# Layer a's last four attention pairs: three couples of contraction tiles in seven products, and a softmax without the row's own gate sum

## The chip, the cores and the metric

The kernel runs on one core of one Trainium2 chip. The metric is the device time of one launch in microseconds (us); three runs of the kernel before gave 2052.01, 2052.78 and 2052.95 us.

## The reference, cut to what matters

Two transformer layers over 256 rows of 2048 numbers, all in float32. Layer a projects to queries, keys, values and a forget gate, attends causally with a bias that is the difference of two running sums of log gates, projects back, and runs a squared-ReLU MLP. Layer b does the same with chunked attention and a learned relative bias. The change is in layer a's projection and attention:

```python
u = rms_norm(h, a_norm_g[l])
proj = u @ a_w_in[l]                      # 256 x 2048 times 2048 x (3*2048 + 16)
q, k, v, fz = jnp.split(proj, [D, 2 * D, 3 * D], axis=-1)
...
logf = jax.nn.log_sigmoid(fz + a_b_f[l])
c = jnp.transpose(jnp.cumsum(logf, axis=1), (0, 2, 1))
...
s = jnp.einsum('bqhd,bkhd->bhqk', qb, kb).astype(jnp.float32) * scale
s = s + c[:, :, q0:q1, None] - c[:, :, None, :q1]
s = jnp.where(causal[None, None], s, -jnp.inf)
p = jax.nn.softmax(s, axis=-1).astype(vb.dtype)
```

The term `c[:, :, q0:q1, None]` is one number per query row; a softmax over the row gives the same result without it.

## The kernel before, in words

**Precision.** Every large product is made three times: each float32 operand is split into a part `hi` that TensorE multiplies in its float32r format and a rest `lo`, and hi·hi, hi·lo and lo·hi are summed. For the weights the split is made on the chip: ScalarE copies a loaded weight tile into `hi` (L323), VectorE subtracts to get `lo` (L324). A weight tile is 128 partitions by 1024: two contraction tiles of 128 by 512 output columns.

**Units.** The program is a long list of units that TensorE works off in written order. A *plain unit* is one weight tile: 2 contraction tiles, 2 halves of the 256 rows, 3 passes, so 12 matmuls of 128x128x512 (L592, L594, L596: the first two passes use `hi`, the third uses `lo`). Panels of 512 output columns are taken in pairs, and a pair needs 16 contraction tiles for each of its two panels.

**Seven products.** In a pair, part of the contraction is done by the seven-product scheme for 2x2 block matrices instead of eight block products. The four blocks are called 11, 12, 21 and 22; sums of blocks T1 to T4 are needed, and a *form* is one of the seven products, in the order 11, T3, T2, T1, 21, T4, 22. T3 = 22 + 12 and T2 = T3 + 11 are made by VectorE (`make`, L970); T1 = 12 + 11 and T4 = T2 + 21 are made by a DMA that adds from HBM into the tile (`put`, L980, on GpSimd's queue). The matching sums of activations lie in tiles `S` (L395 to L405). A *couple* is one contraction tile of the blocks 1x with one of 2x. Attention pairs do two couples in seven products: a form is 6 matmuls, the seven are 42 in place of 48, and the other 12 contraction tiles take 6 plain units for each panel. Pairs of the MLP do four couples, each form in two parts.

**Order.** `Pair.plan` writes the units of a pair in a row, with plain units between forms by the strings of the table ORD ("a3" is plain unit 3 of the first panel, "b4" unit 4 of the second, "F" the next form). `run` follows the list. Ahead of the products of a unit, `top_up` splits the weights of the next ones: at most three `hi`/`lo` pairs exist (pool `wsp`, 3 buffers), and raw weight tiles are loaded about three ahead on the queue of SyncE. After each unit `run` calls `run_fill` as many times as the table HM says; each call issues one slot of other work: head norms, transposes, softmaxes, value products. Tables such as HS say how many plain units ahead of a pair's first form its blocks are loaded and its sums made, in the order 12, 22, 21, 11, T3, T1. A written order is kept on VectorE, ScalarE, TensorE and SyncE, and for GpSimd's arithmetic.

**Layer a's attention.** Twelve panels (four groups of query, key, value) in six pairs: the first pair is plain units only, five follow with two couples each (order "qkv"), then two pairs of the output projection ("out0", "out1"), then the MLP. From the MLP on every fifth weight tile that is loaded, counted from the program's start, goes into a tile of pool tag `z`, which the hidden activations' transposes also use. The softmax of one head (four to a group) works on two halves, 128x128 and 128x256. For each half VectorE adds the scores, the row's own gate sum `cq` and the bias tile (`scalar_tensor_tensor`, L738) and then takes the row maximum (`tensor_reduce`, L740); ScalarE takes the exponential (L746), and VectorE scales by the reciprocal (L749, L751) and transposes (L440). Layer b has no `cq`: there one `tensor_tensor_reduce` for each half (L742) adds, negates and takes the minimum at once. `cq` is made once by two TensorE transposes (L902) and a copy.

## Time and profile before

| what | value |
|---|---|
| median of three runs | 2052.78 us (2052.01 to 2052.95) |
| the profiled execution, its own time | 2049.66 us |
| its span from first to last instruction | 2047.9 us |
| granted TensorE clock, mean | 0.999 |
| attention of layer a in the trace, with the output projection | up to about 425 us |

The page gives for each engine the time in which it was busy; matmuls are pipelined, so that a reported 390 ns of one matmul overlaps the next. The spacing of starts is read from the chain of work that ended last and from the timeline. Idle time of an engine counts only where TensorE, which works nearly all the time, waits for it.

### The profile page before, as it was taken

Reading aid. Unit: us, or ns where it says so; the run is one execution under the profiler, and the core shown is the slowest. Engines: PE = TensorE matmul, PEld = TensorE weight load, DVE = VectorE, ACT = ScalarE, POOL = GpSimd, SP = SyncE. Lnnn points to the kernel's source line nnn. Section 1 sums busy time; section 2 is a strip of 40 time slices with the busy share of each in tenths; the row PEclk is TensorE's granted clock in tenths of the full one; section 3 lists DMA queues with packets and bytes.
Section 4 is the critical chain, followed back from the end, with each engine's and each line's share of the span. In section 5 each row is a group of like instructions: output and inputs, shape, how many; then the busy total and the mean of one; then the engine's idle time right before and its main releaser. Section 6 shows DMA issues by size and latency. Waiting matters only on the chain.

```text
span 2047.9 us, 27097 instructions
## 1 busy us (share of the span) xinstructions
PE 2041.1 (100%) x9062; PEld 1688.5 (82%) x9062; DVE 1783.5 (87%) x2065; ACT 1403.7 (69%) x1805; POOL 245.0 (12%) x351
## 2 busy tenths in 40 slices
PE   9999999999999999999999999999999999999999
PEld 7888888888888888888888888888888888888887
DVE  7788888998898899899988778888988998988996
ACT  7766666677677677677778666667766676776764
POOL 1111110011111102101012111001101111111020
PEclk9999999999999999999999999999999999999999
DMA  8898888998888898898879888888988888888984
GB/s 322 265 298 272 266 280 243 309 278 272 282 262 281 272 293 272 247 292 273 260 242 311 275 254 287 255 264 284 291 291 265 266 270 284 266 284 261 299 259 147
DMA packets 175309, 557.78 MB, mean 272 GB/s; under 512 B 40624, under 2 KB 69184, under 8 KB 152640
## 3 DMA queue, kind: packets, MB, share of 16 engines
q1 hardware_dynamic: 154112, 464.99, 63.9%
q0 software_dynamic: 20768, 90.75, 22.5%
q8 instruction: 71, 1.16, 0.2%
q14 instruction: 70, 0.57, 0.1%
q10 hardware_dynamic: 288, 0.30, 0.1%
HBM read 516.07 MB, written 27.29 MB: 265 GB/s over the span
## 4 chain that ended last, share of the span: by engine, by line
PE 98%; DVE 1%; ACT 1%; issue 0%; DMA 0%; DVEq 0%; ACTq 0%
PE acc L596 23%; PE acc L592 23%; PE acc L594 23%; PE s L592 9%; PE s L594 9%; PE s L596 9%; PE po L729 1%; PE po L766 1%; DVE lo L324 0%; PE po L767 0%; PE po L728 0%; ACT hi L323 0%; DMA gsb<-in_gs 0%; PE pg L868 0%; DVE s L995 0%
## 5 line engine op out<-in xcount | busy, mean ns | idle before, releaser
L324 DVE TENSOR_TENSOR lo<-raw,hi 128x1024 fp32r<-128x1024 f32 (+1 forms) x409 | 493.5, 1211 | 81.5 <-ACT hi L323 77.1
L323 ACT ACTIVATE hi<-raw 128x1024 fp32r<-128x1024 f32 (+1 forms) x409 | 429.5, 1054 | 194.0 <-PE acc L594 123.4
L592 PE MATMUL acc<-hi,act 128*128 128x512 f32 x1774 | 496.3, 393 | 0.7 <-ACT hi L323 0.7
L596 PE MATMUL acc<-lo,act 128*128 128x512 f32 x1774 | 491.1, 390 | 0.7 <-DVE lo L324 0.6
L594 PE MATMUL acc<-hi,act 128*128 128x512 f32 x1774 | 490.7, 389 | 0.0
L596 PEld LDWEIGHTS acc<-lo,act 128*128 128x128 f32 x1774 | 332.5, 188 | 72.1 <-DVE lo L324 3.1
L594 PEld LDWEIGHTS acc<-hi,act 128*128 128x128 f32 x1774 | 333.0, 188 | 70.1 <-DVE act L383 0.5
L592 PEld LDWEIGHTS acc<-hi,act 128*128 128x128 f32 x1774 | 331.2, 188 | 69.6 <-ACT hi L323 2.1
L323 ACT ACTIVATE hi<-w 128x1024 fp32r<-128x1024 f32 x254 | 267.0, 1058 | 124.0 <-PE acc L594 82.7
L324 DVE TENSOR_TENSOR lo<-wT,hi 128x1024 fp32r<-128x1024 f32 x220 | 267.2, 1221 | 66.1 <-ACT hi L323 62.2
L324 DVE TENSOR_TENSOR lo<-w,hi 128x1024 fp32r<-128x1024 f32 x254 | 305.3, 1217 | 14.0 <-ACT hi L323 12.3
L323 ACT ACTIVATE hi<-wT 128x1024 fp32r<-128x1024 f32 x220 | 232.1, 1059 | 102.1 <-PE acc L594 48.5
L592 PE MATMUL s<-hi,act 128*128 128x512 f32 x530 | 146.3, 391 | 0.0
L596 PE MATMUL s<-lo,act 128*128 128x512 f32 x530 | 145.0, 389 | 0.0
L594 PE MATMUL s<-hi,act 128*128 128x512 f32 x530 | 144.8, 388 | 0.0
L466 POOL DMA_DIRECT2D q<-z x192 | 95.7, 510 | 255.1 <-DVE z L440 211.0
L596 PEld LDWEIGHTS s<-lo,act 128*128 128x128 f32 x530 | 99.2, 188 | 20.8 <-DVE lo L324 0.5
L594 PEld LDWEIGHTS s<-hi,act 128*128 128x128 f32 x530 | 99.4, 188 | 20.6
L592 PEld LDWEIGHTS s<-hi,act 128*128 128x128 f32 x530 | 99.1, 188 | 20.2
L592 PE MATMUL s<-hi,S 128*128 128x512 f32 x288 | 89.6, 392 | 0.0
L596 PE MATMUL s<-lo,S 128*128 128x512 f32 x288 | 88.8, 390 | 0.0
L594 PE MATMUL s<-hi,S 128*128 128x512 f32 x288 | 88.7, 389 | 0.0
(217 smaller groups left out, 2284.4 us busy)
## 6 DMA issues: line engine op xcount, KB each, us to landing
raw<-in_w_in SPq DMA_DIRECT2D x75, 512.0 KB, 5.9
w<-in_w2fa SPq DMA_DIRECT2D x32, 1024.0 KB, 6.5
w<-in_w2fb SPq DMA_DIRECT2D x32, 1024.0 KB, 6.2
w<-in_w1fa SPq DMA_DIRECT2D x27, 1024.0 KB, 7.0
w<-in_w1fb SPq DMA_DIRECT2D x27, 1024.0 KB, 7.3
raw<-in_w2sa SPq DMA_DIRECT2D x52, 512.0 KB, 7.0
raw<-in_w2sb SPq DMA_DIRECT2D x50, 512.0 KB, 7.3
raw<-in_w_kv SPq DMA_DIRECT2D x48, 512.0 KB, 5.1
```

The costliest lines, as they stand in the source:

```text
L323: S.activation(hi[:, c], raw[:, c], AF.Copy)
L324: V.tensor_tensor(lo[:, c], raw[:, c], hi[:, c].bitcast(F32), op=ALU.subtract)
L466: (G if i % 2 else SY).dma_start(dst[32 * j : 32 * j + 32, i * n : (i + 1) * n], z[32 * i : 32 * i + 32, j * n : (j + 1) * n])
L592: TE.matmul(ps[:, cols], xh, cut(hi, j), start=first, stop=False, **kw)
L594: TE.matmul(ps[:, cols], xl, cut(hi, j), start=False, stop=False, **kw)
L596: TE.matmul(ps[:, cols], xh, cut(lo, j), start=False, stop=last, **kw)
L729: TE.matmul(s[:, P : 3 * P], q[:, a, P:T], k[:, a], start=True, stop=True)
L766: TE.matmul(po[:, :T], v[:, 0, a * P : (a + 1) * P], pT[:, :2], start=True, stop=False)
```

## The change

1. The last four attention pairs (order "three") do three couples, six contraction tiles, in seven products. Their blocks are 128x1536 (`WIDE`). Each form has a first part of 1024 columns (6 matmuls) and a second, a *half form*, of 512 (3 matmuls); 5 plain units for each panel are left instead of 6. The columns 1024 to 1536 of the four blocks lie beside the others in two tiles of their own (`beside`: a tile `aside` of pool tag "s", and the first half of `h[0]`, which held x and is loaded again from HBM when "out0" opens). T3 and T2 become two VectorE additions each, T1 and T4 two DMAs each.
2. A half form's `hi` and `lo` come from the same three full-size buffers and count as split ahead like any other. Before, halves of this size would have had a buffer of their own; no pair had any.
3. One further sum of activations (`sum_third`) for the third couple, once, early.
4. The softmax of layer a takes layer b's form, one `tensor_tensor_reduce` per half; `cq` and its two transposes are gone.
5. Tables: HM has 153 numbers in place of 133 with the same sum, 113; the pairs "three" get the row "a3 a4 F a5 F a6 b3 a7 F b4" and the times HT, "out0" gets (9, 8, 1, 6, 6, 5).

```diff
-    "HM": (1, 2, 1, 0, 0, 1, 1, 1, 0, 1, 1, 2, 1, 1, 0, 1, 1, 1, 1, 1, 2, 0, 1, 1, 1, 1, 1, 0, 1, 0, 0, 1, 1, 1, 0, 0, 1, 1, 1, 1, 0, 1, 1, 1, 1, 1,
+    "HM": (1, 2, 1, 0, 0, 1, 1, 1, 0, 1, 1, 2, 1, 1, 0, 1, 1, 1, 1, 0, 1, 2, 0, 1, 1, 0, 1, 1, 0, 1, 0, 1, 0, 0, 1, 0, 1, 1, 0, 0, 0, 1, 1, 0, 1, 1,
...
+    "HT": (7, 8, 1, 5, 4, 3),
...
-    "OFH": (11, 10, 2, 7, 7, 6),
+    "OFH": (9, 8, 1, 6, 6, 5),
...
-        "deep0": "a4 F F F b4 a5 a6 a7"},
+        "deep0": "a4 F F F b4 a5 a6 a7", "three": "a3 a4 F a5 F a6 b3 a7 F b4"},
...
+        if three is not None:
+            f, s = three
+            for i in range(f.shape[0] // 4):
+                src = [[None] * 3 + [s[5 * (2 * i + q) + u] for u in range(5)] for q in range(2)]
+                big = {k: f[4 * i + m] for m, k in enumerate(("11", "12", "21", "22"))}
+                j = len(pairs) + 1
+                pairs.append(Pair(big, src, "three", j % 2 == 1, TABLES["HT" if i else "HS"], WIDE))
...
-        hi = wsp.tile([P, n], F32R, name="hi" if n == UN else "hih", bufs=3 if n == UN else 1)
-        lo = wsp.tile([P, n], F32R, name="lo" if n == UN else "loh", bufs=3 if n == UN else 1)
+        hi = wsp.tile([P, UN], F32R, name="hi", bufs=3)[:, :n]
+        lo = wsp.tile([P, UN], F32R, name="lo", bufs=3)[:, :n]
...
-        ready.append((hi, lo, n < UN))
+        ready.append((hi, lo, False))
...
-        tag = "qs"[g // 2]
+        tag = "qs"[g // 2 if layer else 0]
...
-            if cq is not None:
-                V.scalar_tensor_tensor(t[:, c], s[:, c], cq[:, b, g * GH + a : g * GH + a + 1], bias[:, a, c],
-                                       op0=ALU.add, op1=ALU.add)
-                V.tensor_reduce(nm[:, b : b + 1], t[:, c], axis=AX.X, op=ALU.max, negate=True)
-            else:
-                V.tensor_tensor_reduce(out=t[:, c], in0=s[:, c], in1=bias[:, a, c], scale=-1.0, scalar=-3.0 * NEG,
-                                       op0=ALU.add, op1=ALU.min, accum_out=nm[:, b : b + 1])
+            V.tensor_tensor_reduce(out=t[:, c], in0=s[:, c], in1=bias[:, a, c], scale=-1.0, scalar=-3.0 * NEG,
+                                   op0=ALU.add, op1=ALU.min, accum_out=nm[:, b : b + 1])
...
+            if p.wide:
+                p.e[name] = beside(p.rooms[name])
+                SY.dma_start(p.e[name], p.big[name][:, UN:])
...
         V.tensor_tensor(d, a, b, op=ALU.add)
+        if e:
+            V.tensor_tensor(*e, op=ALU.add)
...
         G.dma_start(p.t[name][:, cols], p.big[other][:, cols], accum_op=ALU.add)
+        if p.e:
+            G.dma_start(p.e[name], p.big[other][:, UN:], accum_op=ALU.add)
...
+    def sum_third(x, fs):
+        y = wk.tile([P, 512], F32, name="y3", tag="wk").rearrange("p (a t) -> p a t", a=2)
+        for j in range(2):
+            V.tensor_tensor(y[:, j], x[2 * UA + j][:, 0].bitcast(F32), x[2 * UA + j][:, 1].bitcast(F32), op=ALU.add)
+        yield
+        s = qkv.tile([P, UN], F32R, name="S", tag="s", bufs=2)
+        fs.extend(s[:, i * 512 : i * 512 + 512] for i in range(2))
+        yield from sums([[y[:, j : j + 1, b * P : (b + 1) * P] for j in range(2)] for b in range(NB)], fs[2:], 1)
...
+            if p.order == "out0" and three:
+                SY.dma_start(h[0][:, :UN], xr[0][:, :UN])
```

In the changed program the lines stand some 12 lower: L336 is `lo`, L749 the softmax operation (two instructions, the second writes the row's minimum), L755 and L757 its reciprocal and scaling, L452 the transpose, L986 and L988 the two additions of `make`, L604, L606 and L608 the three passes.

Place one: VectorE, the third of the four pairs, from the `lo` of its second form, T3, to the `lo` of the plain unit behind it. `wT` is the tile of T3 and T2, `R` holds block 11, `pbuf` the softmax's tiles, `raw` a plain unit's weights. Before:

```order
L324 TENSOR_TENSOR lo<-wT_1674,hi 128x1024
L970 TENSOR_TENSOR wT_1674<-wT_1674,R 128x1024
L749 RECIPROCAL row<-row 128x2
L751 TENSOR_SCALAR pbuf<-pbuf,row 128x128
L751 TENSOR_SCALAR pbuf<-pbuf,row 128x256
L440 STREAM_TRANSPOSE pbuf<-pbuf 128x3x4x32
L324 TENSOR_TENSOR lo<-raw,hi 128x1024
```

Now, at the same place (its first rows, up to the softmax operation, whose three further instructions and the `lo` of `raw` follow):

```order
L336 TENSOR_TENSOR lo<-wT_1709,hi 128x1024
L755 RECIPROCAL row<-row 128x2
L757 TENSOR_SCALAR pbuf<-pbuf,row 128x128
L757 TENSOR_SCALAR pbuf<-pbuf,row 128x256
L452 STREAM_TRANSPOSE pbuf<-pbuf 128x3x4x32
L336 TENSOR_TENSOR lo<-wT_1709,hi 128x512
L986 TENSOR_TENSOR wT_1709<-wT_1709,R 128x1024
L988 TENSOR_TENSOR wT_1709<-wT_1709,aside 128x512
L749 ISA t,row<-po,nb 128x128
L749 ISA row 128x1
L749 ISA t,row<-po,nb 128x256
```

The half form's `lo` and the second addition have come in ahead of the plain unit's `lo`, and one operation of the next head's softmax stands there too.

TensorE at that place, the form T3 and the plain unit behind it. `acc` and `s` are PSUM tiles, `S` the sums of activations, `act` the activations. Before:

```order
L592 MATMUL acc_1789<-hi_1797,S_393 128x512 x2
L594 MATMUL acc_1789<-hi_1797,S_394 128x512 x2
L596 MATMUL acc_1789<-lo_1798,S_393 128x512 x2
L592 MATMUL s_1384<-hi_1811,act_296 128x512 x2
L592 MATMUL s_1385<-hi_1811,act_296 128x512 x2
```

Now:

```order
L604 MATMUL acc_1828<-hi_1843,S_393 128x512 x2
L606 MATMUL acc_1828<-hi_1843,S_394 128x512 x2
L608 MATMUL acc_1828<-lo_1844,S_393 128x512 x2
L604 MATMUL acc_1828<-hi_1858,S_811 128x512
L606 MATMUL acc_1828<-hi_1858,S_811 128x512
L608 MATMUL acc_1828<-lo_1859,S_811 128x512
L604 MATMUL s_1406<-hi_1893,act_296 128x512 x2
```

Three matmuls of the half form have come in between the form and the plain unit.

Place two: VectorE, the first of the four pairs, the same stretch and on to the `lo` of the next form. Before:

```order
L324 TENSOR_TENSOR lo<-wT_843,hi 128x1024
L970 TENSOR_TENSOR wT_843<-wT_843,R 128x1024
L324 TENSOR_TENSOR lo<-raw,hi 128x1024
L749 RECIPROCAL row<-row 128x2
L751 TENSOR_SCALAR pbuf<-pbuf,row 128x128
L751 TENSOR_SCALAR pbuf<-pbuf,row 128x256
L440 STREAM_TRANSPOSE pbuf<-pbuf 128x3x4x32
```

Now:

```order
L336 TENSOR_TENSOR lo<-wT_852,hi 128x512
L986 TENSOR_TENSOR wT_852<-wT_852,R 128x1024
L988 TENSOR_TENSOR wT_852<-wT_852,h_90 128x512
L755 RECIPROCAL row<-row 128x2
L757 TENSOR_SCALAR pbuf<-pbuf,row 128x128
L757 TENSOR_SCALAR pbuf<-pbuf,row 128x256
L452 STREAM_TRANSPOSE pbuf<-pbuf 128x3x4x32
L749 ISA t,row<-po,nb 128x128
L749 ISA row 128x1
L749 ISA t,row<-po,nb 128x256
L749 ISA row 128x1
L336 TENSOR_TENSOR lo<-raw,hi 128x1024
```

The softmax work that stood behind the plain unit's `lo` now stands ahead of it.

More of the change, by code (lines that the diff above doesn't have):

```diff
@@ L259, in plan_out, with plan_heads @@
         return plan, [(b, 1, u) for u in (5, 6, 7)]
[L261 removed]
+    def plan_heads(w, when, w_out, rest=None, three=None):
         pairs = []
@@ L337, in half_next @@
         u = raws[0][0] if raws else units[0]
-        return isinstance(u, Form) and u.half and not u.pair.deep
+        return False
     def top_up(ahead=AHEAD, early=EARLY):
@@ L953, in make @@
             elif p.order in LAZY:
-                t[name] = acts.tile([P, 2 * UN], F32, name="wT3", tag="act")[:, :UN]
+                both = acts.tile([P, 2 * UN], F32, name="wT3", tag="act")
+                t[name] = both[:, :UN]
+                if p.wide:
+                    p.e[name] = both[:, UN:WIDE]
             else:
@@ L1197, in heads @@
         base = turns[0]
-        last = next(p for p, q, i in plan_h[::-1] if isinstance(p, Pair) and p.order in LAZY[:2])
-        run(plan_h, opener(x, fs, evacs, o, out, base, last, TABLES["XOH"]), TABLES["HM"], plan_a[0][0])
+        last = next(p for p, q, i in plan_h[::-1] if isinstance(p, Pair) and p.order == "three")
+        step3 = steps(lambda: sum_third(x, fs))
+        add_fill([[]] * TABLES["X3"] + [[step3]] * 4)
+        run(plan_h, opener(x, fs, evacs, o, out, base, last, TABLES["XOH"], True), TABLES["HM"], plan_a[0][0])
         halves_of.clear()
```

64 lines of the change are left out of this document (37 added, 27 removed), and 6 rows, old and new, of the table TABLES.

## The prediction

> **What bounds the kernel now.** I read the busy shares first, then TensorE's waits, then the chain that ended last, and last the single rows of VectorE. The busy line of the page, and the stretch of layer a's attention in the view by windows (columns PE, its weight loads, DVE, ACT, POOL, granted clock, DMA share, GB/s):
>
> ```profile
> PE 2041.1 (100%) x9062; PEld 1688.5 (82%) x9062; DVE 1783.5 (87%) x2065; ACT 1403.7 (69%) x1805; POOL 245.0 (12%) x351
> 46.00:420.00 374.00, 374.00 (x1684) 310.20 (x1683) 317.18 (x445) 249.04 (x404) 49.24 (x53) 1.00 0.86 272
> ```
>
> TensorE (PE) never pauses in those 374 us; VectorE (DVE) is busy 85% of them, ScalarE 67%. All waits of TensorE in the trace:
>
> ```profile
> PE pt L141 <- DVE mhalf L143: 1.0, 1, 1.0
> PE acc L592 <- ACT hi L323: 0.7, 1, 0.7
> PE acc L596 <- DVE lo L324: 0.6, 1, 0.6
> ```
>
> None lies in the attention. So a gain can only be matmuls that are not made, and a loss only a wait that is not there yet. The pace of matmuls, from the chain of work that ended last:
>
> ```profile
> 47.48 0.91 PE acc L592 x4
> ```
>
> Four in 0.91 us, 0.2275 us each.
>
> **The matmuls.** A couple costs 24 matmuls in block products (2 contraction tiles, 2 panels, 2 row halves, 3 passes) and 21 in seven products. Four pairs save 3 each: 12 x 0.2275 = 2.73 us. The two transposes of `cq` go as well:
>
> ```profile
> L902 PE MATMUL pt<-ident,early 16*128 16x16 f32 x2 | 0.3, 218 | 0.0
> ```
>
> That is 0.3 us, all of it on the path, since TensorE has no idle time there. Together 3.03 us. This is the most that the change can give as long as TensorE's pace stays: 2052.78 - 3.03 = 2049.75 us.
>
> **VectorE's prices.** Starts in the timeline show what an operation really takes from VectorE, which is less than its duration (start, us, what):
>
> ```profile
> 297.72 0.16 DVE L749 RECIPROCAL row<-row 128x2 f32<-128x2 f32 x1
> ...
> 299.00 0.12 DVE L749 RECIPROCAL row<-row 128x2 f32<-128x2 f32 x1
> ...
> 304.20 1.21 DVE L970 TENSOR_TENSOR wT<-wB 128x1024 f32<-128x1024 f32 x1
> 305.33 2.35 DVE L324 TENSOR_TENSOR lo<-raw,hi 128x1024 fp32r<-128x1024 f32 x2
> ...
> 272.96 1.28 DVE L405 TENSOR_TENSOR S<-sum,S 128x512 fp32r<-128x512 f32 x2
> 274.17 0.70 DVE L440 STREAM_TRANSPOSE z<-qn 128x512 f32<-128x512 f32 x1
> ```
>
> Reciprocal, scaling and transpose of a head: 1.28 us. An addition or a `lo` of 1024 columns: 1.13 to 1.14. One of 512 columns, the size of the half forms: (274.17 - 272.96)/2 = 0.605. The softmax's sum and maximum of one head, in layer a and in layer b's form:
>
> ```profile
> 290.56 0.34 DVE L738 SCALAR_TENSOR_TENSOR t<-po,cq,nb 128x128 f32<-128x128 f32 x1
> ...
> 291.99 0.34 DVE L738 SCALAR_TENSOR_TENSOR t<-po,cq,nb 128x128 f32<-128x128 f32 x1
> ...
> 1182.40 0.25 DVE L742 CUSTOM_DVE_ANT_0 t<-po,rb 128x128 f32<-128x128 f32 x1
> ...
> 1182.93 0.68 DVE L663 TENSOR_REDUCE ss<-sq 128x4 f32<-128x512 f32 x1
> ...
> 1184.64 1.22 DVE L324 TENSOR_TENSOR lo<-raw,hi 128x1024 fp32r<-128x1024 f32 x1
> ...
> 100.77 0.70 DVE L1020 SCALAR_TENSOR_TENSOR acc<-acc,p 128x512 f32<-128x512 f32 x1 [0.49 <-PE acc L596]
> 101.38 1.22 DVE L324 TENSOR_TENSOR lo<-R,hi 128x1024 fp32r<-128x1024 f32 x1
> ```
>
> 1.43 us become 0.53. (The last three rows price what comes up below: one round of head sums, 1.71 us, and one addition in PSUM, 0.61.) Over the stretch VectorE gets 28 half `lo` for 8 whole ones (16.9 - 9.1 = +7.8), 8 more additions (+4.8) and the third sum (seven operations of at most 512 columns, so at most 7 x 0.605 = 4.2; most are of 128 or 256, so I take half, 2.1); it loses 16 x 0.90 = 14.4. The balance is +0.3 us: the softmax pays for the products in the mean. ScalarE gets 28 half `hi` for 8 whole ones:
>
> ```profile
> L323 ACT ACTIVATE hi<-raw 128x1024 fp32r<-128x1024 f32 x97 | 101.8, 1059 | 32.9 <-PE acc L594 13.1 <-PE s L594 6.4 <-DMA raw<-in_w_oa 3.6
> L402 ACT ACTIVATE S<-sum 128x512 fp32r<-128x512 f32 x6 | 3.6, 627 | 1.2 <-DVE sum L396 1.1
> ```
>
> 28 x 0.627 - 8 x 1.059 = +9 us in 374, from 67% to 69%. I set it at nothing: ScalarE's idle third covers it, unless it comes in one piece.
>
> **Where the cover is thin.** The mean is not what decides. A half form lasts 3 x 0.2275 = 0.68 us on TensorE and asks 0.605 of VectorE; the additions for T2 and one head's softmax now stand ahead of a plain unit's `lo`. Three `hi`/`lo` buffers let VectorE lead; the lead is counted to a unit's third pass, which needs `lo`. In place one (third pair) VectorE has, from the `lo` of T3 to that of the plain unit, 1.28 + 0.605 + 1.14 + 0.605 + 0.53 + 1.14 = 5.30 us of work; TensorE, from third pass to third pass, 2 + 3 + 8 = 13 matmuls, 2.96 us. The lead shrinks by 2.34 us; before, by 3.56 - 2.28 = 1.28. In place two (first pair), from the half of T3 over seven units, to the first plain unit behind T1, VectorE has five whole and two half `lo` (6.9), one T2 (1.75), three softmax ends (3.84), two beginnings (1.06), one addition in PSUM (0.6) and one round of head sums (1.71): 15.9 us, against 51 matmuls and three heads' scores. The rows give the scores' price, and the lead that before could lose without a wait:
>
> ```profile
> 261.82 0.38 PE L728 MATMUL po<-R,q 128*128 128x128 f32 x2
> ...
> 262.29 1.28 PE L592 MATMUL acc<-hi,act 128*128 128x512 f32 x4
> ...
> 260.96 1.21 DVE L324 TENSOR_TENSOR lo<-R,hi 128x1024 fp32r<-128x1024 f32 x1
> ...
> 274.79 1.18 DVE L324 TENSOR_TENSOR lo<-raw,hi 128x1024 fp32r<-128x1024 f32 x1
> ...
> 266.12 0.62 PE L596 MATMUL s<-lo,S 128*128 128x512 f32 x2
> ...
> 276.55 1.07 PE L596 MATMUL s<-lo,act 128*128 128x512 f32 x4
> ```
>
> Scores take 0.47 us a head, so TensorE has 11.6 + 1.41 = 13.0 us in place two, and the lead shrinks by 2.9. From the half of T3 to the plain unit's `lo`, the second pair has 1.75 + 1.14 = 2.9 of work against 9 matmuls and one head's scores, 2.5: 0.4; the fourth, with a softmax end, 4.2 against 2.05: 2.1. In the quoted stretch of before the first `lo` ends at 262.17 for a pass at 266.12 (lead 3.95), the last at 275.97 for 276.55 (0.58): 3.37 us lost, no wait. With a half form among the three buffers a form's lead is at most 0.68 + 2.73 + 0.91 - 1.14 = 3.2 us. So the new waits lie between 0 (each place starts with its full lead) and 2.9 + 0.4 + 2.3 + 2.1 = 7.7 us (no lead anywhere). I take 1.2, near the lower end: the quoted stretch, the nearest row, lost more and had 0.58 left, but its lead was larger.
>
> All this goes by starts. If every operation held VectorE for its whole duration, 0.08 us more (the addition at 304.20 lasts 1.21 us, the next starts after 1.13), the some 50 operations of the four places would take 4.0 us more, and the sum would be 2055.0. The Trainium skill, "VectorE: DVE Perf Modes", section "The DRAIN you can't avoid", has it so: the next operation does not start until the pipe is empty. The rows at 304.20 and 305.33 disagree with it, and the sum above goes by them.
>
> **Queues.** SyncE issues 17 DMAs more (16 for the blocks' extra columns, one for x) and 8 fewer for plain units, GpSimd 8 more; what is added in bytes is 0.5 MB a pair for T1 and T4 and 0.5 MB for x again, 2.5 MB, or 9 us at 272 GB/s in 374 us: the DMA share goes from 0.86 to about 0.88. Deadlines: block 12 is now loaded three plain units and two forms with halves ahead of T3's additions, 3 x 2.73 + 2 x 2.05 = 12.3 us (before five and two, 16.4). The second DMA of T1 and T4 follows the first on GpSimd, and the head norms' power behind it waits one issue longer. The landings of block 12 and its like, of T4, and the issue:
>
> ```profile
> DMA to landing us min/median/max: 3.0/5.8/10.9
> ...
> wT<-in_w_in POOLq DMA_DIRECT2D x5, 512.0 KB, 5.3
> ...
> L980 POOL DMA_DIRECT2D wT<-in_w_in x5 | 4.5, 890 | 53.0 <-DVE lo L324 53.0
> ```
>
> 10.9 is inside 12.3; T4 has a plain unit, T1's form, two plain units and the form 21, 12.3 us too. The 0.9 us fall on the idle third of ScalarE, which waits for the power. I cost all this at nothing. The loads behind a block on SyncE wait for the same `lo` as before, and x is loaded again most of a pair ahead of its reader.
>
> **Sum.** 2052.78 - 3.03 + 1.2 = 2050.95, said as 2051.0 us. The profiled execution took 2049.66 us, 3.1 below the median of the runs; the same step leads there to 2047.8. A difference of 0.2%, 4.1 us, is about what a measurement of this kernel can tell from none.
>
> **Rivals.**
> - No new wait: 2049.75 us. For it: the means balance, and before lost 3.37 us of lead without a wait. Against: place two follows three heads of softmax with smaller buffers in time.
> - Slower: VectorE falls behind at T2 in the four pairs. It decides from 3.03 us of waits on, 0.76 a pair; with the leads wholly absent 2049.75 + 7.7 = 2057.5. For it: idle VectorE time is lost while it waits for ScalarE's exponentials, which my tally leaves out. Against: 15% idle in the mean. Additive durations (2055.0) end here too; against them stand the quoted starts, which come before the ends.
> - Slower by the MLP: eight plain tiles fewer shift by three which loads take a tile of tag `z`, in both layers. The trace's only wait for `lo` stands at the MLP's beginning:
>
> ```profile
> 432.50 0.72 PE L596 MATMUL acc<-lo,act 128*128 128x512 f32 x2 [0.63 <-DVE lo L324]
> ```
>
>   Four or eight such waits more would give 2053.5 to 2056.0. Against: in none of the rows does TensorE wait for a load there.
> - Faster than the matmuls: if the two waits of 0.7 and 0.6 us went too, 2048.45. Against: one is the program's start, which the change does not touch.
>
> **How the numbers follow.** Few waits (0.2 to 2.5 us; 2049.9 to 2052.3), my forecast: 0.53. None: 0.20. VectorE behind, 2052.8 to 2057.5: 0.14, a third of it over 2056.9. Additive durations: 0.03. The MLP: 0.05, seldom over 2056.9. Faster than the matmuls: 0.05. So faster by over 0.2% 0.06, within 0.2% 0.86, slower 0.08. Runs lie 0.5 us to either side, so the range goes from 2049.2 to 2054.5: it leaves out the last case and the upper half of the slow ones. The likeliest case's own range is 2049.4 to 2052.8.
>
> **What the new profile would show.** 12 matmuls of 512 columns fewer on TensorE and its busy time down by 3 us; L742's operation in place of L738 and L740 at 0.53 us a head; VectorE's busy time in the attention about the same. If I am right, TensorE's waits for `lo` add up to about 1 us and stand behind T2 in the first, third or fourth pair. I am wrong if they pass 3 us, if the waits name a DMA or `hi`, or if the MLP after 440 us has new ones.

## The result, and the profile after

The changed kernel took 2073.89 us (median of five runs, 2071.48 to 2077.2); the kernel before, in the same rounds, 2052.01 us. The ratio is 1.0107, with a 95% interval of 1.0092 to 1.0122: slower by 1.1%, 22 us, and far outside the predicted range. The profiled execution of the changed kernel has a span of 2072.1 us, 24.2 more than that of before.

The busy line of the page of the changed kernel, and its costliest waits of TensorE (us in total, times, longest):

```profile
PE 2047.2 (99%) x9048; PEld 1686.5 (81%) x9048; DVE 1786.6 (86%) x2099; ACT 1411.2 (68%) x1826; POOL 253.5 (12%) x359
```

```profile
PE s L604 <- ACT hi L335: 7.6, 3, 4.9
PE acc L604 <- ACT hi L335: 7.3, 9, 1.6
PE acc L608 <- DVE lo L336: 2.2, 5, 0.8
PE po L740 <- DMA R<-turn: 1.1, 1, 1.1
```

There are 14 matmuls fewer, as announced (9062 in the prediction's busy line, 9048 here: twelve and the two transposes). Yet TensorE waits 20.3 us in all where it waited 2.3, and it waits for `hi`, which ScalarE writes: 14.9 us. VectorE's `lo`, on which the prediction had its eye, costs 2.5 (0.6 before). TensorE is also busy 6.1 us longer with fewer matmuls; 18.0 and 6.1 make up the 24.2 but for a rounding.

The attention of layer a in the view by windows, TensorE alone (window, its length, us busy, matmuls, granted clock, DMA share, GB/s); before, TensorE was busy without a gap there:

```profile
46.00:100.00 54.00, 53.02 (x240) 1.00 0.78 254
100.00:150.00 50.00, 47.19 (x210) 1.00 0.92 282
150.00:200.00 50.00, 48.21 (x215) 1.00 0.84 260
200.00:250.00 50.00, 46.48 (x206) 1.00 0.89 272
250.00:300.00 50.00, 44.16 (x188) 0.97 0.83 237
300.00:350.00 50.00, 48.76 (x223) 1.00 0.86 265
```

That is 16.2 us of idle time in 304, spread over all four changed pairs and largest in the fourth. The longer busy time belongs to the same pauses. In the timeline of TensorE (start, us, what, idle time before it):

```profile
268.36 0.40 PE L608 MATMUL acc<-lo,act 128*128 128x512 f32 x1
269.13 1.19 PE L604 MATMUL acc<-hi,act 128*128 128x512 f32 x4 [0.38 <-ACT hi L335]
270.16 1.09 PE L606 MATMUL acc<-hi,act 128*128 128x512 f32 x4
```

Without the pause the row at 269.13 would start 0.23 us behind the one at 268.36, and the next 0.91 us behind that. They start 0.77 and 1.03 us apart, so 0.66 us are lost, of which 0.38 show as idle: this pause costs 0.28 us that the profile counts as busy. I call that the refill; four other pauses (105.53, 134.00, 264.82 and 271.49) have one of 0.28 to 0.31. With 20 waits more than before (23 for 3) that is 5.6 us, and a stretch at half pace behind the longest (below) some 1.6 more; the saved matmuls take 3.0 off. That is an estimate of 4.2 of the 6.1; the rest I can't place.

Two places show the kind. The first is a copy that I call P7 (L1038, L1015 in the kernel before): ScalarE copies the products of T3 out of PSUM. ScalarE before, at that place:

```profile
92.27 1.04 ACT L323 ACTIVATE hi<-raw 128x1024 fp32r<-128x1024 f32 x1
96.02 0.60 ACT L1015 ACTIVATE p<-acc 128x512 f32<-128x512 f32 x1 [2.70 <-PE acc L596]
```

The `hi` of the next plain unit stood ahead of P7. ScalarE now, in the first changed pair, from the `hi` of T3's half form (512 columns) to that of the next plain unit:

```profile
93.51 0.61 ACT L335 ACTIVATE hi<-wT 128x512 fp32r<-128x512 f32 x1
96.81 0.60 ACT L1038 ACTIVATE p<-acc 128x512 f32<-128x512 f32 x1 [2.68 <-PE acc L608]
97.30 1.05 ACT L335 ACTIVATE hi<-raw 128x1024 fp32r<-128x1024 f32 x1
```

ScalarE stands 2.68 us at P7, which needs the products of T3, and only then comes to the `hi` of the plain unit. Before, it stood 2.70 us there, but with that `hi` already written. Now TensorE waits 0.98 us for it, up to 98.40. The same happens once in each pair: 0.98 us at 147.29, 1.63 at 194.25, 1.63 at 243.93. The second place is in the fourth pair, where ScalarE works off several operations behind the eviction of a value product (L776, from PSUM) before it comes to the next `hi`, and TensorE meanwhile:

```profile
279.52 0.38 ACT L776 ACTIVATE act<-po 128x256 fp32r<-128x256 f32 x1 [3.60 <-PE po L773]
280.44 1.15 ACT L414 ACTIVATE S<-sum 128x512 fp32r<-128x512 f32 x2 [0.54 <-DVE row L755]
283.38 1.15 ACT L707 ACTIVATE q<-z,gqk 128x1024 f32<-128x1024 f32 x1 [1.79 <-DMA z<-turn]
284.43 1.06 ACT L672 ACTIVATE sq<-acc 128x512 f32<-128x512 f32 x2
285.38 1.05 ACT L335 ACTIVATE hi<-raw 128x1024 fp32r<-128x1024 f32 x1
```

```profile
281.16 0.39 PE L608 MATMUL s<-lo,S 128*128 128x512 f32 x1
286.49 1.96 PE L604 MATMUL s<-hi,act 128*128 128x512 f32 x4 [4.95 <-ACT hi L335]
288.25 1.91 PE L606 MATMUL s<-hi,act 128*128 128x512 f32 x4
289.95 1.14 PE L608 MATMUL s<-lo,act 128*128 128x512 f32 x4
```

The unit in work is a half form of 0.68 us, so 4.95 us of ScalarE's delay come through to TensorE, and the eight matmuls behind take 3.46 us instead of 1.82.

SyncE stands longer too. Its waits between 46 and 340 us at the reads of turned tiles, before and after:

```profile
SPq L456 <- DMA turn<-pbuf: 15.3, 10, 3.5
SPq L456 <- DMA turn<-z: 7.3, 3, 5.1
```

```profile
SPq L468 <- DMA turn<-pbuf: 42.2, 10, 8.6
SPq L468 <- DMA turn<-z: 24.3, 6, 6.0
```

A read waits for the write of the same tile to memory. Half forms bring no weight load at their place in the list, so I take it that fewer loads stand between the two; no run tests that alone. Loads behind it go out late: ScalarE waits 5.30 us for `raw` at 128.76 and 1.54 at 231.37, and TensorE 1.36 and 1.50 behind that. A wait of 0.63 us for `lo` stands in both traces just behind the attention (432.50 before, 452.18 now) and serves as a marker: up to it 19.7 of the 24.2 us are lost; the MLPs and layer b lose 4.5 more.

### The profile page after: what moved, and what is told of

Its sections match the earlier page's. It is cut to its first block, busy times and chain, and to the rows that moved or that the text cites. A ratio compares the mean times of both kernels' runs of the same rounds, so it can differ in the third digit from the quotient of the medians.

```text
span 2072.1 us, 27175 instructions
## 1 busy us (share of the span) xinstructions
PE 2047.2 (99%) x9048; PEld 1686.5 (81%) x9048; DVE 1786.6 (86%) x2099; ACT 1411.2 (68%) x1826; POOL 253.5 (12%) x359
## 4 chain that ended last, share of the span: by engine, by line
PE 85%; DMA 3%; DVE 2%; ACT 1%; issue 1%; SPq 0%; DVEq 0%; ACTq 0%; POOLq 0%
PE acc L608 20%; PE acc L604 20%; PE acc L606 20%; PE s L604 8%; PE s L606 8%; PE s L608 8%; DVE lo L336 1%; ACT hi L335 1%; PE po L741 1%; PE po L772 1%; DMA raw<-in_w1b 0%; DMA w<-in_w1fb 0%; DMA z<-turn 0%; DMA raw<-in_w_ins 0%; DMA R<-turn 0%
## 5 line engine op out<-in xcount | busy, mean ns | idle before, releaser
L335 ACT ACTIVATE hi<-raw 128x1024 fp32r<-128x1024 f32 (+1 forms) x401 | 420.7, 1053 | 205.0 <-PE acc L606 128.9
L336 DVE TENSOR_TENSOR lo<-raw,hi 128x1024 fp32r<-128x1024 f32 (+1 forms) x401 | 485.0, 1214 | 83.9 <-ACT hi L335 79.2
L604 PE MATMUL acc<-hi,act 128*128 128x512 f32 x1760 | 495.0, 393 | 7.7 <-ACT hi L335 7.3
L608 PE MATMUL acc<-lo,act 128*128 128x512 f32 x1760 | 489.1, 390 | 2.3 <-DVE lo L336 2.0
L606 PE MATMUL acc<-hi,act 128*128 128x512 f32 x1760 | 488.2, 389 | 0.0
L604 PEld LDWEIGHTS acc<-hi,act 128*128 128x128 f32 x1760 | 328.3, 188 | 78.7 <-ACT hi L335 11.4
L608 PEld LDWEIGHTS acc<-lo,act 128*128 128x128 f32 x1760 | 329.5, 188 | 74.8 <-DVE lo L336 6.4
L606 PEld LDWEIGHTS acc<-hi,act 128*128 128x128 f32 x1760 | 330.2, 188 | 69.8 <-DVE act L433 0.5
L336 DVE TENSOR_TENSOR lo<-wT,hi 128x1024 fp32r<-128x1024 f32 (+1 forms) x232 | 274.8, 1194 | 67.0 <-ACT hi L335 61.2
L336 DVE TENSOR_TENSOR lo<-w,hi 128x1024 fp32r<-128x1024 f32 x254 | 305.6, 1219 | 15.5 <-ACT hi L335 14.0
L335 ACT ACTIVATE hi<-wT 128x1024 fp32r<-128x1024 f32 (+1 forms) x232 | 238.8, 1037 | 101.6 <-PE acc L606 51.8
L604 PE MATMUL s<-hi,act 128*128 128x512 f32 (+1 forms) x524 | 146.2, 394 | 7.6 <-ACT hi L335 7.6
L606 PE MATMUL s<-hi,act 128*128 128x512 f32 (+1 forms) x524 | 144.3, 390 | 0.0
L608 PE MATMUL s<-lo,act 128*128 128x512 f32 (+1 forms) x524 | 143.9, 389 | 0.3 <-DVE lo L336 0.3
L604 PEld LDWEIGHTS s<-hi,act 128*128 128x128 f32 x524 | 98.1, 189 | 29.5 <-ACT hi L335 9.5
L608 PEld LDWEIGHTS s<-lo,act 128*128 128x128 f32 x524 | 98.1, 188 | 21.7 <-DVE lo L336 1.7
L606 PEld LDWEIGHTS s<-hi,act 128*128 128x128 f32 x524 | 98.8, 189 | 20.7
L604 PE MATMUL s<-hi,S 128*128 128x512 f32 x296 | 92.2, 390 | 0.0
L608 PE MATMUL s<-lo,S 128*128 128x512 f32 x296 | 91.9, 389 | 0.0
L606 PE MATMUL s<-hi,S 128*128 128x512 f32 x296 | 91.8, 389 | 0.0
```

Source lines behind the costliest of these rows:

```text
L335: S.activation(hi[:, c], raw[:, c], AF.Copy)
L336: V.tensor_tensor(lo[:, c], raw[:, c], hi[:, c].bitcast(F32), op=ALU.subtract)
L604: TE.matmul(ps[:, cols], xh, cut(hi, j), start=first, stop=False, **kw)
L606: TE.matmul(ps[:, cols], xl, cut(hi, j), start=False, stop=False, **kw)
L608: TE.matmul(ps[:, cols], xh, cut(lo, j), start=False, stop=last, **kw)
```

## The experiments

Sixteen kernels. Each median stands beside the ratio to the kernel before, measured in the same rounds (its medians there: 2051.1 to 2053.0 us).

### The softmax, alone

The kernel before with the new softmax; `cq` and its transposes are gone.

```diff
-                V.scalar_tensor_tensor(t[:, c], s[:, c], cq[:, b, ...], bias[:, a, c], op0=ALU.add, op1=ALU.add)
-                V.tensor_reduce(nm[:, b : b + 1], t[:, c], axis=AX.X, op=ALU.max, negate=True)
+            V.tensor_tensor_reduce(out=t[:, c], in0=s[:, c], in1=bias[:, a, c], scale=-1.0, scalar=-3.0 * NEG,
+                                   op0=ALU.add, op1=ALU.min, accum_out=nm[:, b : b + 1])
```

> The kernel before with the one-operation softmax alone, without cq and its two transposes. All theories: VectorE's work falls by about 14 us in the attention, TensorE's by 0.3 us, the time stays within 1 us of before, 2051 to 2053 us. If the softmax were the cause of the loss it would be above 2060.

2051.3 us, ratio 0.9994 (0.9986 to 1.0003): no difference. The loss is in the products.

### A unit split ahead, reads one place later, and both

First run: where a half form comes up, one plain unit more is split before its products. Second: the reads of the turned softmax go one place later in the fill list. Third: both.

```diff
+            if q == 3 and not p.deep:
+                top_up(1)
             hi, lo = ready.popleft()[:2] if q > 1 and ready and not p.deep else fetch()
...
-        st["carry"] = carry(z, st["pT"], 0)
+        st["carry"] = carry(z, st["pT"], 1)
```

> The changed kernel (2073.9 us) with one call of top_up(1) ahead of each half form's products, so that the next plain unit's hi stands on ScalarE ahead of the copy of the accumulator (L1038) that waits for the half form of T3. Copy theory: four waits of 0.98 to 1.63 us behind T3, 5.2 us in all, go, with the slower matmuls behind them: 2067 to 2069 us. Queue theory (late loads behind SyncE's reads of turned tiles): no change beyond 1 us, 2073 to 2075. Lead theory (VectorE too late with lo, the prediction's slower rival): no change either, since VectorE's work and the three buffers stay, 2073 to 2075.

> The changed kernel with the softmax tiles' way through HBM given one more slot between write and read (carry with wait 1 in place of 0), so that more weight loads stand between the two on SyncE. Queue theory: SyncE's waits for its own writes (42 us in the attention against 15 before) fall below 20 us, the late raw loads and the 4.95 us wait go, 2064 to 2067 us. Copy theory: no change beyond 1 us, 2073 to 2075. Lead theory: no change, 2073 to 2075.

> Both edits on the changed kernel. If copy and queue theory each hold for their part: 2058 to 2061 us, and TensorE's waits in the attention fall from 16 us to below 4. If only one holds: as that one alone. Lead theory: 2073 to 2075.

2072.24 us (1.0087, 1.0072 to 1.0103), 2074.45 (1.0102, 1.0088 to 1.0116) and 2071.52 (1.0084, 1.0064 to 1.0104): neither alone nor both give what I expected, and all three intervals overlap that of the changed kernel (1.0092 to 1.0122). The traces say why. With a unit split ahead all four waits at P7 are gone, but TensorE comes to the late loads sooner: the waits behind them grow from 1.36 and 1.50 us to 2.18 (130.49) and 3.47 (234.01). With later reads SyncE's waits for `turn<-pbuf` fall from 42.2 to 16.8 us, those two waits of TensorE are gone, and the four at P7 stay (0.98 at 98.63 and 145.32, 1.63 at 192.33 and 240.43). With both, 46 to 250 us lose 3.2 us of idle time where the changed kernel lost 9.1; but now the third group of heads waits for its own turned softmax tile. TensorE and SyncE in that run:

```profile
276.61 1.19 PE L772 MATMUL po<-pbuf,R 128*128 128x256 f32 x2 [5.92 <-DMA pbuf<-turn]
```

```profile
256.64 8.13 SPq L310 DMA_DIRECT2D raw<-in_w_ins  x3
264.83 1.85 SPq L468 DMA_DIRECT2D z<-turn  x4
266.77 4.08 SPq L468 DMA_DIRECT2D pbuf<-turn  x4
```

The read of `pbuf` stands behind three loads that take 8.13 us, mostly waiting for free tiles. 250 to 300 us alone have 9.2 us of idle time. In one queue either the reads hold up the loads or the loads the reads.

### The reads on another queue

As the first run above, with the softmax's reads issued by GpSimd; then also those of the normed queries and keys.

```diff
-        st["carry"] = carry(z, st["pT"], 0)
+        st["carry"] = carry(z, st["pT"], 0, G)
...
-                turns = [[t] for _, _, _, t in rest] + carry(z, dst)
+                turns = [[t] for _, _, _, t in rest] + carry(z, dst, 1, G)
```

> The split-ahead kernel (2072.2 us) with one more change: the four reads of every turned softmax tile are issued by GpSimd instead of SyncE; their place in the program is that of the changed kernel. In the run with both fixes a read one place later cleared the loads of three pairs, but in the last pair the read of pbuf itself then stood behind three raw loads that took 8.13 us (256.64) and a z read, and TensorE stood 5.92 us and went on at half pace: 9.24 us of that stretch. Queue theory (SyncE is held by reads that wait for their writes, and the loads behind go out late): with neither behind the other, 250 to 300 us loses under 3 us in place of 9.24, the hi waits by late raw loads go, 2059 to 2063. Rival, buffers: the loads are late because raw buffers come free late, whoever issues them: 2069 to 2073, waits that name hi and the raw load stay. Rival, GpSimd's queue: its block additions and the norm's power stand behind a read that waits for its write, 2066 or more with waits on R, wT or qn.

> As the run before, and the reads of the normed query and key tiles (turned z) go to GpSimd too. Queue theory: the 24.3 us that SyncE stood at those six reads go as well, 1 to 3 us less than the run before: 2057 to 2061. Rival, buffers: within 1 us of the run before. Rival, GpSimd's queue: slower than the run before by over 1 us, since each z read waits 5 to 6 us for its write with the other half's power and the additions behind it.

2069.17 us (1.0099, 1.0079 to 1.0119) and 2081.85 (1.0146, 1.0131 to 1.0161). The first can't be told from the run with a unit split ahead alone (2072.24; the intervals overlap) and is far from the 2059 to 2063 of the queue theory. It lies where both rivals had it, late buffers and GpSimd's queue, and doesn't decide between them. The second is the slowest of all variants of the changed kernel, as the rival of GpSimd's queue had it: the norms' power (L680) stands behind reads that wait for their writes. ScalarE's wait for that power was 2.6 us between 46 and 340 us in the changed kernel and 8.0 in the first run; in the second run:

```profile
ACT qn L686 <- POOL ss L680: 15.0, 6, 6.0
```

### The count of loads in the MLP

The fifth weight load that goes into a tile of tag `z` is the same one again as before the change.

```diff
-... if extra[0] and extra[1] % 5 == 0 else ...
+... if extra[0] and (extra[1] + 8) % 5 == 0 else ...
```

> The changed kernel with one number different: which of every five raw tiles of the layers behind is taken from the query buffers' ring is set back to the count that the kernel before had there (the change made eight loads more before it). Theory of the shifted ring: the new waits of the MLP (0.63 us at 452.18, 0.65 at 943.46, 0.23 and 0.83 near 1464 to 1470) go with what follows on them, 3 to 4.5 us in all: 2069.5 to 2071. Rival: those waits come from the extra weight traffic or from the new time at which the stage starts, and stay: 2073 to 2075.

2070.82 us (1.0094, 1.0079 to 1.0109), 3.1 below the changed kernel and within what was expected; but the two intervals overlap, so the trace must bear it out. TensorE from 440 to 1500 us, changed kernel and this run:

```profile
440.00:1500.00 1060.00, 1056.74 (x4676) 1.00 0.88 273
```

```profile
440.00:1500.00 1060.00, 1059.09 (x4689) 1.00 0.89 274
```

3.26 us of idle time become 0.91. That would bear out the rival of the prediction that was given 0.05. Two things speak against taking it as shown. The same execution has 13.3 us of idle time from 46 to 350 us where the changed kernel had 16.2, though the edit changes nothing there, so single executions differ by as much. And with own buffers (the next runs) the old count left the idle time from 440 to 1500 us as it was: 3.00 us with the new count, 2.97 with the old. Over all variants of the changed kernel, idle time from 460 to 1500 us is 0.3 to 2.7 us with the old count and 1.2 to 4.2 with the new. What the count costs stays open.

### Buffers of their own for the halves, and their order

A half's `hi` gets its own tile, its `lo` one of the work ring (two small rings of sums are shorter to make room). A half isn't counted among the units split ahead, so one more full unit may be. The second run keeps the tiles and drops the two lower edits.

```diff
-        hi = wsp.tile([P, UN], F32R, name="hi", bufs=3)[:, :n]
-        lo = wsp.tile([P, UN], F32R, name="lo", bufs=3)[:, :n]
+        hi = wsp.tile([P, n], F32R, name="hi" if n == UN else "hih", bufs=3 if n == UN else 1)
+        lo = wsp.tile([P, UN], F32R, name="lo", bufs=3) if n == UN else wk.tile([P, n], F32R, name="loh", tag="wk")
...
-        ready.append((hi, lo, False))
+        ready.append((hi, lo, n < UN))
...
-        return False
+        return isinstance(u, Form) and u.half and not u.pair.deep
```

> The changed kernel with one change: the halves' hi and lo get buffers of their own (hi a tile of its own, lo one of the work ring) and no longer take two of the three full hi and lo tiles; as in the kernel before, a half isn't counted in the number of units that are split ahead. (Two small rings of sums become shorter to make room.) Theory of the ring: since a half of 0.68 us on TensorE takes the place of a unit of 2.73 us, ScalarE and VectorE run only some 3.4 us ahead where they ran 5.5, and whatever stands in ScalarE's order (the P7 copy, the rows behind a value's eviction near 278) reaches TensorE. Then the waits at the P7 copy (0.98, 0.98, 1.63, 1.63) go and the pauses before the plain units at 243 and 286 shrink: 2058 to 2066. Rival, the queue alone: only the P7 waits go, as in the run that split one unit ahead there: 2070 to 2073. Rival, the work ring: lo of the halves waits for a work tile, and TensorE waits for lo: over 2074.

> The halves' own buffers as in the run that took 2063.9 us, but a half is counted among the units that are split ahead, as in the changed kernel: ScalarE's order is that of the changed kernel, and only the tiles differ. If the loss lies in the order (ScalarE's next unit is written behind the P7 copy and the rows behind a value's eviction), nothing is won: 2071 to 2076, with the waits of 0.98, 0.98, 1.63 and 1.63 us for hi. If it lies in the tiles (the hi of the next unit waits until TensorE has left a full tile that a half holds), 2063 to 2067.

2063.89 us (1.0059, 1.0044 to 1.0074): 10.0 us less than the changed kernel, the largest single step. With the same tiles but the old order, 2071.82 (1.0095, 1.0080 to 1.0110). So 7.9 of the 10.0 us go with the order; the 2.1 between the changed kernel and the second run lie inside the intervals. The order edit moves VectorE's `lo` along with ScalarE's `hi`; I put the gain down to ScalarE because the waits that went name `hi`. ScalarE in the first of the two runs, at the place shown above:

```profile
92.10 0.62 ACT L335 ACTIVATE hih<-wT 128x512 fp32r<-128x512 f32 x1
92.62 1.05 ACT L335 ACTIVATE hi<-raw 128x1024 fp32r<-128x1024 f32 x1
97.21 0.60 ACT L1038 ACTIVATE p<-acc 128x512 f32<-128x512 f32 x1 [3.54 <-PE acc L608]
```

The plain unit's `hi` now stands ahead of the copy. The waits for `hi` are gone from the attention (14.9 us become 0.7 in the whole trace); what TensorE waits for most is another thing:

```profile
PE po L740 <- DMA R<-turn: 6.4, 2, 4.3
PE po L772 <- DMA pbuf<-turn: 1.8, 2, 1.5
```

In the second, TensorE waits at P7 again (0.98 us at 99.79, 0.21 at 147.70, 1.69 at 195.09, 1.63 at 243.12). SyncE still stands 43.0 and 25.1 us at the reads in the first, as much as in the changed kernel, and ScalarE waits 12.6 us for weight loads between 46 and 340 us (10.3 in the changed kernel), but TensorE has no wait for `hi` there. I read it so that ScalarE now does its work a unit earlier and has time for a late load. This one order takes away both kinds of wait that the first three runs could only take away apart.

### The cause, put into the kernel before

One unit less split ahead in the attention pairs of the kernel before; no halves, no more traffic.

```diff
-            hi, lo = ready.popleft()[:2] if q > 1 and ready and not p.deep else fetch()
+            hi, lo = ready.popleft()[:2] if q > 1 and ready and not p.deep else fetch(AHEAD - (p.order == "qkv"))
...
-                        top_up(AHEAD - 1)
+                        top_up(AHEAD - 1 - (p.order == "qkv"))
```

> The kernel before with one unit less split ahead in the attention pairs (one behind the unit in work, where it has two), and nothing else: no halves, no more traffic, no other count of loads. ScalarE's copy P7 then stands ahead of the next unit's hi, as in the changed kernel. If lead in ScalarE's order is what the change lost: waits of TensorE for hi and lo at the P7 copies and behind the values' evictions, 10 to 30 us in all, since a whole unit less is more than the changed kernel lost: 2062 to 2082. If the halves' own work or traffic was the cause and the lead is spare: 2050 to 2055.

2080.29 us (1.0136, 1.0111 to 1.0161), within what was expected. TensorE's waits, and ScalarE at the first P7:

```profile
PE acc L592 <- ACT hi L323: 10.7, 11, 1.6
PE s L592 <- ACT hi L323: 6.6, 7, 1.6
PE acc L596 <- DVE lo L324: 3.1, 5, 1.7
```

```profile
91.32 1.04 ACT L323 ACTIVATE hi<-wT 128x1024 fp32r<-128x1024 f32 x1
98.04 0.60 ACT L1015 ACTIVATE p<-acc 128x512 f32<-128x512 f32 x1 [5.68 <-PE acc L596]
98.53 1.05 ACT L323 ACTIVATE hi<-raw 128x1024 fp32r<-128x1024 f32 x1
```

P7 stands ahead of the plain unit's `hi` again, and TensorE waits the same 1.63 us behind it at 99.64, 201.96 and 252.13. Less lead alone makes such a loss, and here too most of the waiting is for `hi` (17.3 us), little for `lo` (3.3).

### Putting the cures together

Six runs. (1) A unit split ahead, the old count, later reads in the first two groups of heads. (2) Own halves in place of the unit split ahead. (3) As (2), with one step of the output pair's sums earlier. (4) Own halves and the old count, reads as in the changed kernel. (5) As (4), with scores one place later in two groups. (6) As (5), with the later reads.

```diff
-        st["carry"] = carry(z, st["pT"], 0)
+        st["carry"] = carry(z, st["pT"], int(g < 2))
...
-    "XOH": (7, 13, 12, 11),
+    "XOH": (7, 13, 11, 10),
...
-    "ATA": ((10, 13, 15, 19, 9), (9, 12, 15, 18, 12), (8, 13, 15, 19, 9), (9, 9, 12, 12, 9)),
+    "ATA": ((10, 13, 15, 19, 9), (10, 12, 15, 18, 12), (8, 13, 15, 19, 9), (10, 10, 12, 12, 9)),
```

> The changed kernel with a unit split ahead at the half of T3, the old count in the MLP's ring, and the reads of the turned softmax one place later in the first two groups of heads alone (in the third the later read cost 5.92 us at 276.61 and half pace behind it). Queue theory with a place-dependent cost: 46 to 250 us as in the run with both (about 3.3 us idle, mostly at 150 to 200), 250 to 300 as without the later read (3 to 5 us idle), the MLP 2.4 us better: 2059 to 2064. Rival (late reads and early reads cost the same where buffers come late): 2067 to 2071.

> As the run before, with the halves' own buffers in place of the unit split ahead. If ring, queue and count are three separate causes, their gains add: 2051 to 2058. If ring and queue are one cause (both only give the loads more time), 2058 to 2063, no better than the better of the two runs before it by more than 2 us.

> As the run with own halves, old count and later reads (2062.2 us), with one step of the output pair's sums three places of the fill list earlier, so that ScalarE writes S while it waits 3.15 us for the value product at 262.7 to 265.9, and no longer behind it, ahead of q, the squares and hi. If ScalarE's burst there starts the chain squares, power, transposes, turn of the keys that TensorE waited for (1.91 us at 290.92) and the hi behind it, 2 to 4 us less: 2058 to 2060. If the turn's own write and read (6.4 and 7.6 us) set it, within 1 us of 2062.

> The halves' own buffers with their order, and the old count of the MLP's ring; the reads of the turned softmax stand where the changed kernel has them. If the reads on SyncE cost nothing once ScalarE's order is mended: 2059 to 2062, the 2063.9 us of own halves alone less the 2.4 to 3 of the count. If they still hold loads back, 2062 to 2065, and the run below it (all three, 2062.2) is the better by over 1 us.

> As the run before, and the scores of the first head in the second group and of the first two heads in the last group stand one place later in the fill list (first positions 10 for 9), one unit of products of 2.73 us further behind the keys' turn. If TensorE's waits for R<-turn (2.07 and 4.34 us in the run with own halves, with 0.3 us of refill and half pace behind each) are what is left: 3 to 6 us less than the run before, 2054 to 2058. If the late keys are only the last link of a chain that then shows elsewhere (pbuf<-turn, hi), within 1.5 us of it.

> As the run before, with the reads of the turned softmax one place later in the first two groups. If the reads cost nothing once the order is mended: within 1.5 us of the run before. If they hold loads back: 1.5 to 4 us less, 2051 to 2056.

| run | us, median | range of runs | ratio, 95% interval |
|---|---|---|---|
| 1 | 2066.07 | 2062.86 to 2071.09 | 1.0076 (1.0058 to 1.0093) |
| 2 | 2062.21 | 2056.58 to 2062.97 | 1.0043 (1.0027 to 1.0059) |
| 3 | 2057.69 | 2055.19 to 2062.93 | 1.0025 (1.0014 to 1.0037) |
| 4 | 2060.92 | 2057.98 to 2063.28 | 1.0042 (1.0030 to 1.0053) |
| 5 | 2058.46 | 2054.64 to 2065.54 | 1.0030 (1.0019 to 1.0042) |
| 6 | 2056.98 | 2051.03 to 2060.26 | 1.0024 (1.0014 to 1.0033) |

Run 1 fell between its two expectations. Runs 2 and 4 agree: with ScalarE's order mended, later reads change nothing that these intervals show (nor do runs 5 and 6), so no run shows SyncE's queue as a cause of its own. Run 4 is 3.0 below own halves alone, but the intervals overlap, and in the two traces the whole gain lies ahead of the marker (437.32 for 441.62), where the count changes nothing. Run 3 landed where I expected, but not in the way: ScalarE's write of S came no earlier than the end of TensorE's products that it waited for.

```profile
268.87 1.15 ACT L414 ACTIVATE S<-sum 128x512 fp32r<-128x512 f32 x2 [5.54 <-PE s L606]
```

Whether it is faster than run 2 is open: the intervals overlap, and the profiled executions of the two, with spans of 2055.9 and 2054.8 us, don't show it. Run 5 took the keys' wait at 157 us away, the one near 299 stayed at 3.18 us (in the longest of its ten executions, 2065.54), and the gain of 2.5 us is inside the intervals.

Run 6 has the lowest median (run 3 can't be told from it), and is still 0.24% over the kernel before. In its profiled execution (span 2052.8, below its median) the attention is nearly free of pauses, and the marker behind it is back where it was:

```profile
432.73 0.73 PE L608 MATMUL acc<-lo,act 128*128 128x512 f32 x2 [0.63 <-DVE lo L336]
```

432.73 against 432.50: the 3.0 us of saved matmuls just pay for the five pauses that are left, 1.4 us from 46 to 350 us, and their refills. Behind it the MLPs and layer b take 4.7 us more than before (2052.8 - 432.73 against 2047.9 - 432.50), of which 2.0 are more idle time from 440 to 1500. What causes that, and the spread of 9 us between its runs, the experiments don't settle. No version beat the kernel before.

## Why the prediction was wrong

- **The matmuls.** Right: 14 fewer. They don't show in TensorE's busy time, which rose by 6.1 us, because the pauses' refills count as busy; they show in run 6, where the attention ends as early as before in spite of its pauses.
- **The softmax and VectorE's prices.** Right: no difference alone, and VectorE's busy time rose by 3.1 us in the whole span. New waits for `lo` between 46 and 350 us are four, of 1.0 us together; 1.2 were forecast. That the two agree is partly luck: only the first (105.53) stands behind T2, the third pair, which was to lose 2.34 us of lead, has none, and TensorE's waits for `hi` came in between, so that the lead was not run down in the way that was worked out. With own halves and their order no wait for `lo` is left there, but VectorE's lead is then a unit longer too. No run tests that lead alone.
- **Rivals on VectorE.** Neither its falling behind at T2 nor additive durations made the loss. The Trainium skill, "VectorE: DVE Perf Modes", section "The DRAIN you can't avoid", lets an operation start only when the one before it has left the pipe, but adds that a next operation which is not held starts earlier. So the starts at 304.20 and 305.33 speak against the first half alone, and not, as the prediction has it, against the section. The rival built on the first half ended on the right side, but TensorE's 1.0 us of waits for `lo` in the attention speak against it.
- **ScalarE, the step that failed.** "I set it at nothing: ScalarE's idle third covers it, unless it comes in one piece." The price, 9 us, was about right (busy time rose by 7.5). But ScalarE works in written order, and what counts is where the next `hi` stands in it. The prediction counted the three buffers for VectorE's lead alone and asked nowhere what stands ahead of a `hi` and whom that row waits for. The answer was to be read in the listing of ScalarE: since a half of 0.68 us counts as a unit of 2.73, the copy P7, waiting for TensorE itself, slid ahead of the next plain unit's `hi`. In place of nothing it cost up to 10.0 us by the run with own buffers, 7.9 of them by the order alone.
- **The queues.** "I cost all this at nothing. The loads behind a block on SyncE wait for the same `lo` as before" failed too. It looked at loads behind blocks, and not at loads behind the reads of turned tiles, whose waits grew from 22.6 to 66.5 us. Its cost doesn't add to that of ScalarE's order: it showed where the P7 waits were taken away, and was not seen any more once the order was mended.
- **The MLP.** The ring's shift was named and priced at 2.5 to 5 us above the forecast, at a chance of 0.05. The layers behind the attention did lose 4.5 us, but the runs don't show that the count was the cause: with the old count one trace had 2.4 us less idle time there, another had no less. The wait at 432.50 on which the prediction built this rival is in every trace, unchanged at 0.62 or 0.63 us, with the old count and the new.
- **What was in no sum.** A pause costs about 0.28 us beyond its idle time, and some are followed by half pace for a few us. The prediction's bound of 7.7 us for waits had neither.
- **The conditions.** "I am wrong if they pass 3 us, if the waits name a DMA or `hi`, or if the MLP after 440 us has new ones": the last two came. The waits for `lo` stayed below 3 us, at 2.5 in the whole trace.

In medians, of 22 us lost: 10.0 went with own buffers and their order, 3.0 lie between that run and run 4 (the count, which the traces don't bear out), 3.9 went with later scores and reads together (runs 4 to 6, whose intervals just overlap), and 5 are left without a shown cause.

## What to carry to other kernels

A look-ahead that is counted in units shrinks in time when a unit becomes shorter: count it in microseconds, and list for each engine in order what now stands ahead of the operand that the bound engine needs next, above all rows that wait for the bound engine itself. An engine idle a third of the time covers nothing while it stands at such a row. Where curing one wait brings no time, look at once for the wait that took its place, and cure both in one run before dropping either. And where an edit is judged by one trace, check how much the stretches that it doesn't touch have moved.

## What the runs showed of the hardware

- **A pause costs more than its idle time.** At 269.13 us it is 0.66 us for 0.38 shown; five pauses of 0.21 to 0.38 us in that trace each cost 0.28 to 0.31 us more than they show.
- **Half pace behind pauses that are not long.** Behind 4.95 us of idle time eight matmuls ran at 0.44 and 0.43 us each instead of 0.2275, and the granted clock (the third number from the right) was half:

```profile
287.00:290.00 3.00, 3.00 (x9) 0.50 0.98 292
```

  The Trainium skill, "TensorE: Matmul & The Clock Gate", section "What's actually happening", lets TensorE fall to half rate after at least one idle window of about 3.4 us. That agrees with this pause. It does not with the following one, of run 2 above, where 1.91 us were enough (near half pace from 291.2 to 294.8, the granted clock again 0.50), and the measurement decides:

```profile
290.92 0.46 PE L740 MATMUL po<-R,q 128*128 128x128 f32 x2 [1.91 <-DMA R<-turn]
291.22 0.79 PE L741 MATMUL po<-R,q 128*128 128x256 f32 x2
291.80 0.64 PE L740 MATMUL po<-R,q 128*128 128x128 f32 x2
292.23 1.06 PE L741 MATMUL po<-R,q 128*128 128x256 f32 x2
292.73 2.27 PE L604 MATMUL acc<-hi,act 128*128 128x512 f32 x4
```

```profile
292.00:294.00 2.00, 2.00 (x8) 0.50 1.04 414
```

  Nor is a pause of 3 us always followed by it: with the softmax's reads on GpSimd one of 3.04 us ahead of 282.57 had full pace behind it (granted clock 1.00 from 282 to 286), and with own buffers in the old order one of the same 3.04 us ahead of 283.90 had half pace (0.50 from 284 to 288). The length of the last pause alone does not decide.
